# RWKV block inverse: products of 64x64 in two quarters of the array in place of block-diagonal products of 128x128

## The chip, the core and the metric

The kernel runs on one core of a Trainium2 chip. The metric is the time of one execution in device microseconds. The engines are named as in the profile: PE is TensorE's matrix products, PEld its loads of weights, DVE is VectorE, ACT is ScalarE, POOL is GpSimd, SP is SyncE, which issues the transfers. TensorE's array has 128 rows and 128 columns; rows belong to the partitions of the operands, columns to the partitions of the result. A product whose operands stand in partitions 0 to 63 and whose result goes to partitions 0 to 63 uses one quarter of the array; one from 64 to 127 into 64 to 127 uses the opposite quarter.

## The reference

Two model blocks follow each other over 512 tokens of width 1024. The first is a convolution and an attention layer with their feed-forward layers, the second mixes three things (sliding attention, attention to a memory, and RWKV) and has a feed-forward layer behind it. The change concerns the RWKV mixer alone: six heads of 64 channels, over each of which runs a recurrence of a 64x64 state.

```
def rwkv7_scan(r, w, k, v, a, bvec):
    decay = jnp.exp(-jnp.exp(w))
    def step(state, inp):
        r_t, d_t, k_t, v_t, a_t, b_t = inp
        sa = jnp.einsum('bhvk,bhk->bhv', state, a_t)
        state = (state * d_t[:, :, None, :] + sa[..., None] * b_t[:, :, None, :]
                 + v_t[..., None] * k_t[:, :, None, :])
        return state, jnp.einsum('bhvk,bhk->bhv', state, r_t)
    _, y = lax.scan(step, s0, xs)
```

Around it: `w`, `a` and the gate come from small projections, the result is normalized per head, scaled, gets a bonus term, is multiplied by the gate, and goes through the rows of `w_out` that belong to it.

## The kernel before

The kernel is one program that a scheduler orders. Instructions of each engine are taken in an order that comes from the order in the code, priorities and modelled times; buffers are handed out in that order too. All products here are of fp32 operands, and TensorE does each of them as two instructions, each with its load of weights.

The recurrence is done in chunks of 64 tokens. Eight chunks make the 512 tokens; two chunks make a block of 128 tokens, so there are four blocks (`b`), and two chunks (`q`) in each. Six heads are worked on as three pairs (`i` is the pair, `e` the head in the pair). For each pair:

- `prep(i)` makes the operands: two projections (L1212, L1216), activations and exponentials on ScalarE (with loads of tables in between: L1214, L1218, L1223, L1234), a scan, and transposes (L1264).
- `grams(i)` makes for every block four matrices of 64x64 for each chunk by products of 64 rows (L1398), and takes them out of PSUM under a mask (L1401). The mask writes them as block-diagonal 128x128 matrices: chunk 0 in the upper left, chunk 1 in the lower right, zeros elsewhere. So each block and head has a tile NM of 128x512. L1404 makes a product with one of them, L1402 and L1403 on GpSimd prepare the matrix to be inverted and the start of its inverse XT, and L1409 transposes XT into X.
- `level(o, l)`, five times, doubles the size of the blocks already inverted. For each head three groups of four products, one for each block, 128x128 by 128x128: P1 (L1424: NM by X, taken out under a mask as T by VectorE, L1425), P2 (L1430: XT by T, taken out as the new X by ScalarE, L1432; not in the last level) and P3 (L1436: T by XT, taken out as the new XT by VectorE, L1438).
- `finish(i)` applies the inverse (L1445), makes the chunks' transition matrices (L1454, L1461 to L1463), runs the recurrence over chunks (L1479 and L1480, six steps, each a product and an operation on VectorE), adds up the output in one bank of PSUM (L1485, L1487, L1492), and normalizes it (L1494 to L1517).

The work around it sets the order: `w_out_attention` (products into `wo`, lines L161 to L165 by its helper) stands early in the code with low priority, and fills TensorE beside the first pair's levels. The second pair's levels run beside the first pair's `finish`, the third pair's beside the second's; the last `finish` has nothing beside it. `w_out_add` multiplies the three pairs' results by their rows of `w_out`, which `w_out` loads into NM buffers and splits in two (L1543 to L1547). PSUM has banks `mm` (2), `aux` (2), `rw` (3) and `wo` (1) in this part. The masks stand in one constant array (`rwc`).

Of the kernel before, what the change touches and what calls it, by code (L numbers as in the profile page):

```python
# [57 lines left out]
def _build(ctx, tc, ins, out, stop, dbg):  # L58
# [1213 lines left out]
    with sub("e_x", "xp"), sub("e_w", "wp"), sub("e_t", "sm"):  # L1272
# [34 lines left out]
        for n, (name, i) in enumerate(order):  # L1307
# [12 lines left out]
            if name in ("l", "r", "k", "v"):  # L1320
                shifted(u, {"r": 0, "k": 3, "v": 6, "l": 9}[name] + i, lora if name == "l" else rkv[name][i])
                if n == PREPN:
# [5 lines left out]
                    for c, w in ((640, 512), (1152, 448), (1600, 384)):  # L1328
                        rc.append(tmp()[:, :w])
                        sp.dma_start(out=rc[-1], in_=ins["rwc"][:, c : c + w])  # L1330
                    m4k, eye64, pair = rc[0], rc[1][:, 0:64], rc[1][:, 64:192]
                    lev = [rc[1][:, 192 + 128 * i : 320 + 128 * i] for i in range(2)] + [rc[2][:, 128 * i : 128 * i + 128] for i in range(3)]
# [44 lines left out]
    def rw():  # L1377
        return ps(512, tag="rw")

    def nmt(dt=F32):  # L1380
        return wk(512, "NM", 18, dt=dt)

    def grams(i, o):
        o.NM, o.X, o.XT = [], [], []
        for e in range(2):
            hr = slice(64 * e, 64 * e + 64)
            NM = []
            XT = wk(512, f"XT{e}", 3)
            pk = ps(256, tag="aux")
            for b in range(4):  # L1390
                c = slice(b * 128, (b + 1) * 128)
# [3 lines left out]
                for x, s in ((o.kt, 0), (o.bt, 128)):  # L1395
                    for q in range(2):
                        ch = slice(b * 128 + 64 * q, b * 128 + 64 * q + 64)
                        pe.matmul(p[64 * q : 64 * q + 64, s : s + 128], x[hr, ch], o.AR[hr, b, :, 64 * q : 64 * q + 64], start=True, stop=True)  # L1398
# [6 lines left out]
                NM.append(nm)  # L1405
            X = wk(512, f"X{e}", 2)
            pt = rw()
            for b in range(4):
                pe.transpose(pt[:, b * 128 : (b + 1) * 128], XT[:, b * 128 : (b + 1) * 128], ident)  # L1409
            act.copy(out=X, in_=pt)  # L1410
            act.copy(out=o.RH[:, :, e, 64:128], in_=pk.rearrange("p (t c) -> p t c", t=4))
# [304 lines left out]
```

## Time and profile before

| what | value |
|---|---|
| median of three runs | 2374.22 us (2371.76 to 2375.54) |
| profiled execution | 2373.74 us |
| its span | 2372.0 us |
| TensorE busy (PE) | 2279.0 us, 96% |
| VectorE busy (DVE) | 1644.5 us, 69% |
| ScalarE busy (ACT) | 942.7 us, 40% |
| GpSimd busy (POOL) | 170.9 us, 7% |
| chain that ended last | PE 88%, DVE 5%, ACT 3%, DMA 2% |

The span runs from the first to the last instruction that the profile shows; 1.74 us lie around it. A busy TensorE is not one at its peak, since products overlap in it: how long a group of products takes is read from the start of one group to the start of the next. RWKV work stands between about 1736 and 1993 us, a ninth of the span.

### The profile page before, as it was taken

The numbers are of one execution on the slowest core, as the hardware profiler recorded it, in microseconds if no ns is written. First come the engines' busy times: TensorE is split into PE (matmuls) and PEld (weight loads), VectorE is DVE, ScalarE is ACT, GpSimd is POOL, SyncE is SP. The second block draws the span as 40 slices with busy tenths as digits, with TensorE's granted clock in tenths as the row PEclk, the third lists the DMA queues.
The fourth block names the chain that finished last, engine by engine and source line by source line (L and its number), as shares of the span: only waits on it lengthen the run. The fifth ranks groups of instructions, "written<-read, shape, count | busy, mean of one in ns | idle before, by whom it ended". The sixth has DMA issues, their size and how long they took to land.

```text
span 2372.0 us, 34287 instructions
## 1 busy us (share of the span) xinstructions
PE 2279.0 (96%) x13910; PEld 1885.8 (80%) x13910; DVE 1644.5 (69%) x2634; ACT 942.7 (40%) x1616; POOL 170.9 (7%) x246
## 2 busy tenths in 40 slices
PE   5999899999999999899999999998989999999999
PEld 2777588888888888766789999987768786788887
DVE  4889769867677768666687777676645546767666
ACT  3222633223332235566653433355633323433332
POOL 0000000000000000344300000001431100000000
PEclk8999999999999999999999999999999999999999
DMA  8455323323233211421132322222200002232221
GB/s 314 168 206 172 139 115 116 124 99 107 90 128 112 98 54 55 129 68 36 54 118 78 124 74 106 72 73 68 66 23 23 5 28 105 87 106 90 89 89 54
DMA packets 51385, 229.02 MB, mean 97 GB/s; under 512 B 6395, under 2 KB 11164, under 8 KB 32796
## 3 DMA queue, kind: packets, MB, share of 16 engines
q1 hardware_dynamic: 51228, 226.84, 27.8%
q8 instruction: 109, 1.79, 0.3%
q14 instruction: 48, 0.39, 0.1%
HBM read 213.84 MB, written 6.68 MB: 93 GB/s over the span
## 4 chain that ended last, share of the span: by engine, by line
PE 88%; DVE 5%; ACT 3%; DMA 2%; issue 1%; POOL 0%; SPq 0%; DVEq 0%; ACTq 0%; POOLq 0%
PE mm L161 23%; PE mm L163 23%; PE mm L165 23%; PE po L909 1%; PE aux L905 1%; PE mm L576 1%; PE rw L1436 1%; PE rw L1430 1%; PE rw L1424 1%; DMA raw<-in_ada 1%; PE aux L370 1%; PE sc L887 1%; PE mm L783 1%; PE sc L888 1%; PE aux L402 1%
## 5 line engine op out<-in xcount | busy, mean ns | idle before, releaser
L161 PE MATMUL mm<-xh,wh 128*128 128x512 f32 (+2 forms) x2336 | 658.4, 338 | 15.2 <-ACT xh L479 4.7
L163 PE MATMUL mm<-xl,wh 128*128 128x512 f32 (+2 forms) x2336 | 660.9, 337 | 3.1 <-DVE xl L219 2.1
L165 PE MATMUL mm<-xh,wl 128*128 128x512 f32 (+2 forms) x2336 | 659.7, 337 | 1.9 <-DVE wl L144 1.9
L143 ACT ACTIVATE wh<-raw 128x1024 fp32r<-128x1024 f32 x263 | 274.8, 1057 | 543.3 <-PE mm L163 491.9
L161 PEld LDWEIGHTS mm<-xh,wh 128*128 128x128 f32 x2336 | 409.5, 190 | 70.5 <-ACT xh L479 6.8
L163 PEld LDWEIGHTS mm<-xl,wh 128*128 128x128 f32 x2336 | 410.8, 190 | 55.5 <-DVE xl L219 3.1
L165 PEld LDWEIGHTS mm<-xh,wl 128*128 128x128 f32 x2336 | 410.7, 190 | 49.2 <-DVE wl L144 2.8
L144 DVE TENSOR_TENSOR wl<-raw,wh 128x1024 fp32r<-128x1024 f32 x263 | 324.2, 1242 | 44.5 <-ACT wh L143 40.0
L161 PE MATMUL mm<-gh,wh 128*128 128x512 f32 (+1 forms) x704 | 253.7, 368 | 2.2 <-ACT gh L288 2.0
L163 PE MATMUL mm<-gl,wh 128*128 128x512 f32 (+1 forms) x704 | 254.8, 368 | 0.0
L165 PE MATMUL mm<-gh,wl 128*128 128x512 f32 x704 | 254.0, 367 | 0.0
L249 DVE TENSOR_TENSOR u<-mm,R 128x256 f32<-128x256 f32 x88 | 37.5, 426 | 178.5 <-PE mm L165 176.7
L161 PEld LDWEIGHTS mm<-gh,wh 128*128 128x128 f32 x704 | 131.3, 188 | 26.1 <-ACT gh L288 2.4
L165 PEld LDWEIGHTS mm<-gh,wl 128*128 128x128 f32 x704 | 131.3, 189 | 23.4
L163 PEld LDWEIGHTS mm<-gl,wh 128*128 128x128 f32 x704 | 131.3, 189 | 23.0 <-DVE gl L289 0.3
L310 DVE SCALAR_TENSOR_TENSOR hl<-mm,mod,hl 128x512 f32<-128x512 f32 x176 | 131.3, 747 | 21.1 <-PE mm L165 20.5
L288 ACT ACTIVATE gh<-cv 128x512 fp32r<-128x512 f32 (+1 forms) x66 | 46.5, 705 | 243.0 <-DVE cv L286 243.0
L271 DVE SCALAR_TENSOR_TENSOR cv<-u,vec,cv 128x512 f32<-128x512 f32 (+1 forms) x132 | 110.4, 837 | 9.9 <-ACT cv L262 9.2
L553 DVE SCALAR_TENSOR_TENSOR accp<-v,dwt,accp 128x798 f32<-128x798 f32 (+2 forms) x118 | 113.9, 975 | 2.6
L272 DVE SCALAR_TENSOR_TENSOR cv<-u,vec,cv 128x512 f32<-128x512 f32 (+1 forms) x132 | 110.6, 839 | 3.1
L284 ACT ACTIVATE cv<-cv 128x512 f32<-128x512 f32 (+1 forms) x66 | 46.4, 704 | 118.2 <-DVE cv L272 118.0
L396 DVE SCALAR_TENSOR_TENSOR ac<-ra,sc,ac 128x512 f32<-128x512 f32 x112 | 81.8, 744 | 1.4 <-DMA ra<-in_ada 1.4
(470 smaller groups left out, 3092.2 us busy)
## 6 DMA issues: line engine op xcount, KB each, us to landing
raw<-in_up SPq DMA_DIRECT2D x63, 1024.0 KB, 4.9
raw<-in_dn SPq DMA_DIRECT2D x33, 1024.0 KB, 4.8
raw<-in_ada SPq DMA_DIRECT2D x24, 1024.0 KB, 6.3
ra<-in_ada SPq DMA_DIRECT2D x48, 512.0 KB, 3.6
raw<-in_pw SPq DMA_DIRECT2D x12, 1024.0 KB, 6.2
S<-vd SPq DMA_DIRECT2D x28, 407.0 KB, 5.0
raw<-in_w_in SPq DMA_DIRECT2D x17, 512.0 KB, 3.5
raw<-in_qkv SPq DMA_DIRECT2D x6, 1024.0 KB, 5.0
```

The source lines that it names most:

```text
L143: act.activation(out=hi, in_=part, func=AF.Copy)
L144: dve.tensor_tensor(out=lo, in0=part, in1=hi, op=ALU.subtract)
L161: pe.matmul(p, whi[:, c], xhi[:, s], start=first, stop=False)
L163: pe.matmul(p, whi[:, c], xlo[:, s], start=False, stop=False)
L165: pe.matmul(p, wlo[:, c], xhi[:, s], start=False, stop=last)
L271: dve.scalar_tensor_tensor(out=cv[:, 0:CW], in0=u[:, 0:CW], scalar=wv[0], in1=cv[:, 0:CW], op0=ALU.mult, op1=ALU.add)
L272: dve.scalar_tensor_tensor(out=cv[:, 0:CW], in0=u[:, 2 : 2 + CW], scalar=wv[2], in1=cv[:, 0:CW], op0=ALU.mult, op1=ALU.add)
L284: act.activation(out=ca[:, 0:CW], in_=ca[:, 0:CW], func=AF.Silu)
L288: act.activation(out=gh[:, 0:CW], in_=cb[:, 0:CW], func=AF.Copy)
L310: dve.scalar_tensor_tensor(out=hs, in0=p, scalar=g2[i][:, m : m + 1], in1=hs, op0=ALU.mult, op1=ALU.add)
L396: dve.scalar_tensor_tensor(out=a, in0=t[:, q, :], scalar=sc2[:, k, n : n + 1], in1=a, op0=ALU.mult, op1=ALU.add)
L553: dve.scalar_tensor_tensor(out=acc[:, a:b], in0=x, scalar=w, in1=acc[:, a:b], op0=ALU.mult, op1=ALU.add)
```

## The change

The two chunks of a block are no longer put into one block-diagonal matrix. Chunk 0 stays in partitions 0 to 63, chunk 1 in 64 to 127, both in the same 64 columns, so T, X, XT, the masks and the gram matrices are half as wide (256 columns for four blocks instead of 512; one NM tile of 128x1024 for a head instead of four of 128x512). Each product of 128x128 becomes two of 64x64, one in the upper left quarter of the array and one in the lower right. `bq` lists the eight chunks with their partitions. `grams` takes its products out of PSUM two blocks at a time, GpSimd prepares a head's four blocks at once, and the transposes become products with the identity. In `finish`, products over both chunks become one for each; Q and the output of even and odd chunks get tiles of their own, and the part of the output that needs the state (L1492 before, L1496 after) has its own tile `pc` in a bank of `rw`, which is added on VectorE. `w_out` loads its weights in one piece of 1024 columns.

```diff
@@ grams
+    hs = [slice(0, 64), slice(64, 128)]
+    bq = [(b, hs[q], slice(b * 64, b * 64 + 64)) for b in range(4) for q in range(2)]
...
-                nm = nmt()
-                both = p.rearrange("p (m c) -> p m c", c=64).unsqueeze(2).to_broadcast([128, 4, 2, 64])
-                dve.tensor_tensor(out=nm.rearrange("p (m q c) -> p m q c", m=4, q=2), in0=both, in1=m4k.rearrange("p (m q c) -> p m q c", m=4, q=2), op=ALU.mult)
-                pool.tensor_tensor(out=nm[:, 256:384], in0=nm[:, 256:384], in1=ident, op=ALU.add)
-                pool.tensor_tensor(out=XT[:, c], in0=nm[:, 256:384], in1=pair, op=ALU.mult)
-                pe.matmul(pk[:, b * 64 : (b + 1) * 64], nm[:, 0:128], o.VT[:, b * 128 + 64 * e : b * 128 + 64 * e + 64], start=True, stop=True)
...
-                pe.transpose(pt[:, b * 128 : (b + 1) * 128], XT[:, b * 128 : (b + 1) * 128], ident)
+                if b % 2:
+                    dve.tensor_tensor(out=nm[:, b * 256 - 256 : b * 256 + 256].rearrange("p (b x) -> p b x", b=2), in0=p2.rearrange("p (b x) -> p b x", b=2),
+                                      in1=m4k.unsqueeze(1).to_broadcast([128, 2, 256]), op=ALU.mult)
+            pool.tensor_tensor(out=NM[:, :, 2], in0=NM[:, :, 2], in1=eye64.unsqueeze(1).to_broadcast([128, 4, 64]), op=ALU.add)
+            XT = wk(256, f"XT{e}", 3)
+            pool.tensor_tensor(out=c4(XT), in0=NM[:, :, 2], in1=pair.unsqueeze(1).to_broadcast([128, 4, 64]), op=ALU.mult)
+            for b, r, c in bq:
+                pe.matmul(pk[r, c], NM[r, b, 0], o.VT[r, b * 128 + 64 * e : b * 128 + 64 * e + 64], start=True, stop=True)
...
+            for b, r, c in bq:
+                pe.matmul(pt[r, c], XT[r, c], ident[r, r], start=True, stop=True)
@@ level
-                pe.matmul(p[:, c], NM[b][:, 256:384], X[:, c], start=True, stop=True)
-            dve.tensor_tensor(out=v4(T), in0=v4(p), in1=lev[l].unsqueeze(1).to_broadcast([128, 4, 128]), op=ALU.mult)
+                pe.matmul(p[r, c], NM[r, b, 2], X[r, c], start=True, stop=True)
+            dve.tensor_tensor(out=c4(T), in0=c4(p), in1=lev[l].unsqueeze(1).to_broadcast([128, 4, 64]), op=ALU.mult)
...
-                    pe.matmul(p[:, c], XT[:, c], T[:, c], start=True, stop=True)
-                o.X[e] = wk(512, f"X{e}", 2)
+                    pe.matmul(p[r, c], XT[r, c], T[r, c], start=True, stop=True)
+                o.X[e] = wk(256, f"X{e}", 2)
...
-                pe.matmul(p[:, c], T[:, c], XT[:, c], start=True, stop=True)
-            o.XT[e] = wk(512, f"XT{e}", 3)
+                pe.matmul(p[r, c], T[r, c], XT[r, c], start=True, stop=True)
+            o.XT[e] = wk(256, f"XT{e}", 3)
@@ finish
-                pe.matmul(pq[hs[e], c], G[e][:, b, 0:64], o.NM[e][b][:, 384:512], start=True, stop=True)
+                pe.matmul(pq[n % 2][hs[e], c], G[e][r, b, 0:64], o.NM[e][r, b, 3], start=True, stop=True)
...
-                pe.matmul(py[hs[e], c], G[e][:, b, 64:128], o.NM[e][b][:, 384:512], start=True, stop=False)
+                pe.matmul(py[n % 2][hs[e], c], G[e][r, b, 64:128], o.NM[e][r, b, 3], start=True, stop=False)
...
-                        pe.matmul(py[hs[e], nn], S[hs[e], nn], QT[hs[e], nn], start=False, stop=n % 2 == 1)
-        act.copy(out=y, in_=py)
+        for q in range(2):
+            act.copy(out=half(y, q), in_=c4(py[q]))
+        pc = rw()
+        for n in range(1, 8):
+            for e in range(2):
+                pe.matmul(pc[hs[e], n * 64 : n * 64 + 64], S[hs[e], n * 64 : n * 64 + 64], QT[hs[e], n * 64 : n * 64 + 64], start=True, stop=True)
+        dve.tensor_tensor(out=y[:, 64:512], in0=pc[:, 64:512], in1=y[:, 64:512], op=ALU.add)
@@ w_out
-            raw = nmt()
-            sp.dma_start(out=raw, in_=ins["w_ob"][n][:, c * 512 : (c + 1) * 512])
+        raw, hi, lo = nmt(), nmt(F32R), nmt(F32R)
+        sp.dma_start(out=raw, in_=ins["w_ob"][n])
```

Line numbers move by a few: after the change P1 is L1430, P2 L1435 and P3 L1440, the recurrence's product is L1482, its part of the output L1496.

The scheduler orders the new program anew. TensorE in the first pair's levels, between two runs of `w_out_attention` products (`wo`); before:

```order
L165 MATMUL wo<-oh,wl 128x512
L1430 MATMUL rw<-T_16731,XT_16708 128x128 x4
L1436 MATMUL rw<-XT_16708,T_16731 128x128 x4
L1424 MATMUL rw<-X_16722,NM 128x128 x4
L161 MATMUL wo<-oh,wh 128x512
L163 MATMUL wo<-ol,wh 128x512
```

The same place of the changed program:

```order
L165 MATMUL wo<-oh,wl 128x512
L1435 MATMUL rw<-T_16747,XT_16712 64x64 x8
L1440 MATMUL rw<-XT_16712,T_16747 64x64 x8
L1430 MATMUL rw<-X_16734,NM 64x64 x8
L1264 MATMUL aux<-ident,AR 128x128 x4
L1264 MATMUL aux<-ident,bt 128x128 x4
L161 MATMUL wo<-oh,wh 128x512
```

The three groups of a level still stand together between two runs of wide products; each has eight products of 64x64 in place of four of 128x128.

TensorE where the second pair's levels run beside the first pair's recurrence (`aux<-f` is a step of it, `f` are its tiles); before, products of 128x128 and of 64x64 alternate:

```order
L1430 MATMUL rw<-T_17304,XT_16963 128x128 x4
L1436 MATMUL rw<-XT_16963,T_17304 128x128 x2
L1479 MATMUL aux<-f 64x64 x2
L1436 MATMUL rw<-XT_16963,T_17304 128x128 x2
L1424 MATMUL rw<-X_17051,NM 128x128 x4
L1479 MATMUL aux<-f 64x64 x2
L1492 MATMUL mm<-f 64x64 x2
L1430 MATMUL rw<-T_17325,XT_17011 128x128 x4
L1436 MATMUL rw<-XT_17011,T_17325 128x128 x4
L1424 MATMUL rw<-X_17316,NM 128x128 x2
L1479 MATMUL aux<-f 64x64 x2
L1492 MATMUL mm<-f 64x64 x2
```

After the change, from the point where the first two steps have been done:

```order
L1496 MATMUL rw<-f 64x64 x4
L1430 MATMUL rw<-X_17100,NM 64x64 x8
L1482 MATMUL aux<-f 64x64 x2
L1496 MATMUL rw<-f 64x64 x2
L1435 MATMUL rw<-T_17440,XT_17089 64x64 x8
L1440 MATMUL rw<-XT_17089,T_17440 64x64 x5
L1482 MATMUL aux<-f 64x64 x2
L1496 MATMUL rw<-f 64x64 x2
L1440 MATMUL rw<-XT_17089,T_17440 64x64 x3
L1430 MATMUL rw<-X_17145,NM 64x64 x8
L1482 MATMUL aux<-f 64x64 x2
L1496 MATMUL rw<-f 64x64 x2
```

All rows here are now of 64x64, and the steps of the recurrence are set between or into the groups of a level.

VectorE in the last `finish`, from Q (L1465, L1469 after) to the subtraction of the mean (L1497, L1500 after); L1547 is a split of `w_out` weights, L1480 (L1483 after) a step of the recurrence; before:

```order
L1465 TENSOR_TENSOR f<-mm,AR 128x512
L1469 TENSOR_TENSOR f<-mm,t 128x4x64
L1474 TENSOR_TENSOR f<-mm,lend 128x4x64
L1469 TENSOR_TENSOR f<-mm,t 128x4x64
L1474 TENSOR_TENSOR f<-mm,lend 128x4x64
L1547 TENSOR_TENSOR NM<-NM 128x512
L1480 SCALAR_TENSOR_TENSOR f<-aux,lend,f 128x64 x3
L1547 TENSOR_TENSOR NM<-NM 128x512
L1480 SCALAR_TENSOR_TENSOR f<-aux,lend,f 128x64 x3
L1497 SCALAR_TENSOR_TENSOR f<-mm,f 128x512
```

After:

```order
L1469 TENSOR_TENSOR f<-rw,AR 128x4x64 x2
L1472 TENSOR_TENSOR f<-mm,t 128x4x64
L1477 TENSOR_TENSOR f<-mm,lend 128x4x64
L1472 TENSOR_TENSOR f<-mm,t 128x4x64
L1477 TENSOR_TENSOR f<-mm,lend 128x4x64
L1483 SCALAR_TENSOR_TENSOR f<-aux,lend,f 128x64 x6
L1497 TENSOR_TENSOR f<-rw,f 128x448
L1500 SCALAR_TENSOR_TENSOR f<-mm,f 128x512
```

The two splits have moved ahead, to the levels before, and the 448-column add (L1497 after) has come in behind the last step.

## Rows read from the trace of the kernel before

**Rows 1.** Stretches of RWKV work: busy us of each engine (instructions), granted TensorE clock, DMA.

```profile
1755.00:1833.50 78.50, 75.50 (x535) 63.87 (x535) 45.23 (x68) 26.21 (x46) 18.99 (x33) 0.98 0.10 30
1833.50:1863.30 29.80, 28.30 (x319) 24.97 (x319) 9.16 (x19) 5.18 (x10) 0.00 (x0) 1.00 0.03 11
1863.30:1867.90 4.60, 4.56 (x26) 2.92 (x25) 1.67 (x3) 1.22 (x2) 0.00 (x0) 1.00 0.00 0
1867.90:1901.40 33.50, 29.50 (x218) 23.85 (x218) 20.43 (x35) 15.52 (x23) 8.29 (x13) 0.93 0.00 1
1901.40:1932.20 30.80, 30.07 (x340) 26.53 (x339) 13.86 (x27) 8.95 (x16) 2.69 (x6) 0.97 0.17 53
1932.20:1952.70 20.50, 17.44 (x134) 15.14 (x133) 12.08 (x18) 4.82 (x8) 0.00 (x0) 1.00 0.00 1
1952.70:1969.40 16.70, 14.40 (x215) 12.15 (x214) 5.80 (x14) 2.65 (x5) 0.00 (x0) 1.00 0.05 18
```

**Rows 2.** Groups of instructions, 1735 to 1995 us: busy us, mean ns of one, idle before.

```profile
L1425 DVE TENSOR_TENSOR T<-rw,t 128x512 f32<-128x512 f32 x30 | 20.7, 690 | 12.5 <-PE rw L1424 12.1
...
L1462 PE MATMUL mm<-T,q 64*64 64x64 f32 x64 | 8.5, 218 | 0.0
...
L1404 PE MATMUL aux<-q,NM 128*128 128x64 f32 x32 | 6.2, 281 | 2.9 <-DVE NM L1401 2.9
...
L1469 DVE TENSOR_TENSOR f<-mm,t 128x256 f32<-128x256 f32 x6 | 2.5, 423 | 9.8 <-PE mm L1463 9.8
...
L1411 ACT COPY RH<-aux 128x256 f32<-128x256 f32 x6 | 2.2, 370 | 13.0 <-PE aux L1404 12.9
```

**Rows 3.** Chain that ended last, third pair's levels: start us, us, what.

```profile
1937.57 1.13 PE rw L1430 x8
1938.70 0.89 PE rw L1436 x8
1939.60 0.91 PE rw L1424 x8
...
1940.53 0.70 DVE T L1425
...
1941.36 1.13 PE rw L1430 x8
```

**Rows 4.** TensorE in order of time, last recurrence: start, from first start to last end.

```profile
1963.84 0.33 PE L1479 MATMUL aux<-f 64*64 64x64 f32 x4 [0.39 <-DVE f L1480]
...
1964.56 0.33 PE L1479 MATMUL aux<-f 64*64 64x64 f32 x4 [0.27 <-DVE f L1480]
1964.72 0.28 PE L1492 MATMUL mm<-f 64*64 64x64 f32 x4
1964.93 0.44 PE L1485 MATMUL mm<-NM,T 128*64 128x128 f32 x4
1965.20 0.39 PE L1487 MATMUL mm<-NM,q 128*64 128x128 f32 x4
1965.52 0.33 PE L1479 MATMUL aux<-f 64*64 64x64 f32 x4
1965.69 0.28 PE L1492 MATMUL mm<-f 64*64 64x64 f32 x4
```

**Rows 5.** TensorE in order of time, products of one quarter behind each other.

```profile
1956.01 0.28 PE L1462 MATMUL mm<-T,q 64*64 64x64 f32 x2
1956.13 0.28 PE L1463 MATMUL mm<-q 64*64 64x64 f32 x2
```

**Rows 6.** TensorE in order of time, second pair's grams.

```profile
1815.79 0.78 PE L1404 MATMUL aux<-VT,NM 128*128 128x64 f32 x6
```

**Rows 7.** Chain that ended last, from `prep` of the third pair to its grams.

```profile
1869.09 1.28 ACT L1214
...
1880.14 0.19 ACT rn L1234
...
1891.93 0.58 PE mm L1398 x8
```

More of the change, by code (lines that the diff above doesn't have):

```diff
@@ L1327, in _build @@
                     rc = []
-                    for c, w in ((640, 512), (1152, 448), (1600, 384)):
+                    for c, w in ((640, 512), (1152, 192)):
                         rc.append(tmp()[:, :w])
                         sp.dma_start(out=rc[-1], in_=ins["rwc"][:, c : c + w])
-                    m4k, eye64, pair = rc[0], rc[1][:, 0:64], rc[1][:, 64:192]
-                    lev = [rc[1][:, 192 + 128 * i : 320 + 128 * i] for i in range(2)] + [rc[2][:, 128 * i : 128 * i + 128] for i in range(3)]
+                    m4k, eye64, pair = rc[0][:, 0:256], rc[0][:, 256:320], rc[0][:, 320:384]
+                    lev = [rc[0][:, 384 + 64 * i : 448 + 64 * i] for i in range(2)] + [rc[1][:, 64 * i : 64 * i + 64] for i in range(3)]
                 if name == "l":
@@ L1443, in finish @@
             p = rw()
-            for b in range(4):
-                pe.matmul(p[:, b * 128 : (b + 1) * 128], o.XT[e][:, b * 128 : (b + 1) * 128], o.RH[:, b, e], start=True, stop=True)
-            g = wk(512, f"T{e}", 2)
+            for b, r, c in bq:
+                pe.matmul(p[r, b * 128 : (b + 1) * 128], o.XT[e][r, c], o.RH[r, b, e], start=True, stop=True)
+            g = wk(512, f"G{e}", 1)
             act.mul(out=g, in_=p, mul=-1.0)
             G.append(v4(g))
-        hs = [slice(0, 64), slice(64, 128)]
-        pq, pzx = ps(512), [ps(512), ps(512)]
-        for b in range(4):
-            c = slice(b * 128, (b + 1) * 128)
+        half = lambda x, q: x.rearrange("p (b q c) -> p b q c", b=4, q=2)[:, :, q]
+        pq, pzx = [rw()[:, 0:256] for _ in range(2)], [ps(512), ps(512)]
+        for n, (b, r, c) in enumerate(bq):
             for e in range(2):
-                pe.matmul(pq[hs[e], c], G[e][:, b, 0:64], o.NM[e][b][:, 384:512], start=True, stop=True)
+                pe.matmul(pq[n % 2][hs[e], c], G[e][r, b, 0:64], o.NM[e][r, b, 3], start=True, stop=True)
         for e in range(2):
@@ L1464, in finish @@
         QT = ftmp()
-        dve.tensor_tensor(out=v4(QT), in0=v4(pq), in1=o.AR[:, :, 1], op=ALU.add)
+        for q in range(2):
+            dve.tensor_tensor(out=half(QT, q), in0=c4(pq[q]), in1=o.AR[:, :, 1, 64 * q : 64 * q + 64], op=ALU.add)
         AT = ftmp()
-        half = lambda x, q: x.rearrange("p (b q c) -> p b q c", b=4, q=2)[:, :, q]
         for q in range(2):
@@ L1538, in w_out @@
     def w_out(n, x):
-        hi, lo = [], []
-        for c in range(2):
-            raw = nmt()
-            sp.dma_start(out=raw, in_=ins["w_ob"][n][:, c * 512 : (c + 1) * 512])
-            hi.append(nmt(F32R))
-            lo.append(nmt(F32R))
-            act.activation(out=hi[c], in_=raw, func=AF.Copy)
-            dve.tensor_tensor(out=lo[c], in0=raw, in1=hi[c], op=ALU.subtract)
+        raw, hi, lo = nmt(), nmt(F32R), nmt(F32R)
+        sp.dma_start(out=raw, in_=ins["w_ob"][n])
+        act.activation(out=hi, in_=raw, func=AF.Copy)
+        dve.tensor_tensor(out=lo, in0=raw, in1=hi, op=ALU.subtract)
         return hi, lo, x
@@ L1553, in w_out_add @@
             for i, (hi, lo, x) in enumerate(parts):
[L1554 removed]
+                mm3([(p, slice(0, 512))], (hi, lo), x, i == 0, i == len(parts) - 1, m * 128)
             dve.tensor_tensor(out=hl[m], in0=p, in1=hl[m], op=ALU.add)
```

62 lines of the change are left out of this document (26 added, 36 removed).

## The prediction

> **What bounds the kernel now.** I read the stretches of the RWKV part first, then the groups of its instructions, then the chain that ended last, and last the order of time on TensorE, where a start tells more than a busy time does. Only the RWKV part (1755 to about 1993 us) changes; what comes after it starts earlier by what this part saves. There TensorE is busy 75.5 of 78.5 us up to the first `finish`, 28.3 of 29.8 and 30.07 of 30.8 in the two stretches in which `finish` runs beside the next pair's levels, but 17.44 of 20.5 and 14.4 of 16.7 us towards the end [rows 1]. So two limits alternate: TensorE's own work, and the wait between two products in which VectorE takes T out of PSUM. The chain shows that wait plainly: eight instructions each of L1430 (P2), L1436 (P3) and L1424 (P1) in 1.13, 0.89 and 0.91 us, then 0.70 us of L1425 (T) with nothing else on the chain, and the next P2 3.79 us after the last [rows 3].
>
> **What the change is worth in TensorE time.** A product of fp32 is two instructions. A group of four 128x128 products (8 instructions) holds TensorE 0.89 us [rows 3], 0.11 us an instruction. After, the group is 16 instructions of 64x64 with 64 columns. In one quarter of the array two such instructions together last 0.28 us where one lasts 0.218 [rows 2, 5]: they start 0.06 us apart, and pairs follow each other 0.117 us apart [rows 5], 0.058 us an instruction. The question is whether the two chunks, which sit in opposite quarters (rows and columns 0 to 63, rows and columns 64 to 127), run at once. L1492 already does this with its two heads: four instructions, two in each of two opposite quarters, also last 0.28 us [rows 4], so the four start within the same 0.06 us: the second quarter costs nothing. A group of 16 is then 8 pairs by 0.058 = 0.47 us, against 0.89: 0.42 less. There are 3 pairs of heads x 2 heads x (5 + 4 + 5) = 84 such groups in `level`: **35.5 us**. In `grams`, six of L1404's 128x64 instructions last 0.78 us, one 0.28 [rows 2, 6], so 0.10 us from one to the next; 6 groups of 8 become 16 quarter instructions, 0.80 to 0.47: **2 us**. The transposes L1409 (4 instructions, 0.45 us) become 16 quarter ones (0.47), and L1445, L1454, L1485 and L1487 keep their time, since half the rows doubles their number: nothing.
>
> **Changes of shape.** When TensorE goes from one shape of weights to another it pays. L1487's four instructions of 128x64, 0.27 us after L1485's four, are followed by the 64x64 of L1479 after 0.32 us instead of 0.22 (four instructions in two pairs, 0.11 a pair); L1479's four take 0.17 instead of 0.117; and from L1492 to L1485 pass 0.21 instead of 0.117 [rows 4]. So a change costs about 0.10 us before and 0.05 behind it, 0.15 in all. I expected more of them, since the levels leave the shape of the wide products around them. The order says the opposite: from the first gram product to the first `w_out_add` product 131 changes become 69, because now `grams`, `level`, `finish` and the state recurrence all have one shape (up to the first `finish` 39 become 35, between the first and second 45 become 24, then 32 and 7, 15 and 3). 62 x 0.15 = **9 us**. TensorE's work falls by 46.5 us in all.
>
> **The evictions.** T and XT go from 512 columns in 0.690 us (L1425) to 256, X likewise; 256 columns cost 0.423 us on VectorE (L1469) and 0.370 on ScalarE (L1411) [rows 2]. NM's 24 evictions become 12 of the same 512 columns. This frees some 24 us of VectorE, which is not the bound; it counts only where T is waited for. There the cycle of a head and level is P2 1.13 (0.89 and 0.24 of a late first instruction and its tail), P3 0.89, P1 0.91, T 0.70 and 0.16 of hand-overs, 3.79 us [rows 3]. After: P2 0.47 + 0.24, P3 0.47, P1 0.48, T 0.42 and 0.16, **2.25 us**.
>
> **What it adds.** `y` is now copied before the recurrence ends, and a 448-column add (estimate 0.6 us, between 0.423 and 0.690 [rows 2]) takes the place of the last copy (128x512 on ScalarE, estimated 0.6 us from the 0.370 of 256 columns): nothing. `pc` holds one of the three `rw` banks while the recurrence runs; the levels beside it have two, so P1 waits for ScalarE's copy of X behind P2: 0.71 + 0.37 + 0.16 = 1.24 us where P2 and P3 together take 0.55 + 0.47. That is 0.2 us a cycle, three cycles in each of two stretches: 1.3 us at most, 0 at least (where T is late anyway); I take 0.7 in each. GpSimd's 48 short operations become 12 of 256 columns in two steps behind all of a head's NM; the `w_out_attention` products stand behind them in the first pair, the last levels of the pair before in the others. The w_ob loads and casts are all ahead of the third pair's levels, where two casts stood in the last recurrence on VectorE: some of the 16.7 us there, not counted apart.
>
> **The sum, by stretch** [rows 1]. *To the first finish, 78.5 us*: TensorE-bound with `w_out_attention` as filler. 28 groups x 0.42 + 4 gram groups x 0.33 + 4 changes x 0.15 = 13.7, and the two last waits for T get shorter: 14. *finish beside the levels, 29.8 us*: L1445 1.75 (16 instructions at 0.11), L1454 0.9 (8), 48 products of L1461 to L1463 x 0.117 = 5.6, L1485 and L1487 1.9 (pairs of quarters 0.117 apart), then P1 and three cycles with the recurrence in them 0.5 + 6.75, the add and its hand-overs 1.5, the last gap 0.7 of `rw`: 19.6. Saves 10. *4.6 us to the next pair's L1212*: the two 512-column products stay (2.1), 2.5 groups become one: saves 1.7. *33.5 us to the second finish*: here the savings go. From L1212 on, ScalarE has nothing but tables and activations one behind another from 1869.09 to 1880.33, and VectorE's chain of operand preparation runs to 1891.93 [rows 7]. Neither is halved; only five T and XT evictions in it (0.27 each) and one P2 and P3 (0.42 each) are: saves 2.2, although TensorE has 8 us less to do. *30.8 us*: as the 29.8, and more groups move behind it: 19.6, saves 11. *20.5 us*: more levels are left for this stretch (19 groups instead of 14): two wide products 2.1, L1502 and L1510 1.4, four groups and two changes of shape 2.3, a T with its hand-overs 1.2, four cycles 9.0, the last P3, P1 and T 1.8, the last XT 0.6: 18.4, saves 2.1. *16.7 us*: no filler; 1.75 + 0.9 + 5.6 + 1.9 + 4.5 steps of the recurrence at 0.72 (from one L1479 to the next [rows 4]) + 1.5 = 15: saves 1.7. `w_out_add` behind it is unchanged. Together 42.6.
>
> From this I take 2 us for the clock: it was 1.00 in most stretches and 0.93 and 0.97 in two [rows 1], and the stretch behind L1212 will have TensorE idle for a third of it. So 41 us. The profiled execution, 2373.74 us (span 2372.0 and 1.74 around it), becomes 2332.7; the median of the three runs is 0.5 above it: **2333 us**.
>
> **Rivals.** *The recurrence and T waits eat more* (chance 14 in 100). If the stretches behind the first `finish` follow their chains and get only the evictions, about 0.27 us in each of some 25 waits, 7 us, and half of the saved changes, 4 us, with the 14 of the first stretch: 25 us, 2349. For it: these stretches already have idle TensorE at the end. Against: 28.3 of 29.8 and 30.07 of 30.8 us were work.
>
> *The two quarters do not run at once* (5 in 100). 16 instructions of 0.058 are 0.93 us, 0.04 more than now: 84 x 0.04 = 3 us lost, the changes of shape give 9, T waits 4: 2364. L1492 speaks against it, though it shows runs of four instructions, and now runs of 16 to 80 follow. The Trainium skill's page TensorEngine Tiling (Array Packing), section Restrictions and Gotchas, says that different row tiles cannot access the same PSUM bank at the same time. By that rule this rival would hold, as both chunks of a block go to the same bank here, and the time would be the 2364 above. L1492 writes both its quarters to one bank, with the times above, so the trace does not bear the rule out.
>
> *Slower* (3 in 100). A stretch made only of quarter products might let TensorE's clock fall to 1.2 GHz. Behind the first `finish` about 65 us of TensorE's work would be of that kind (56 groups x 0.47, three times 11.8 in `finish`, 4 in `grams`); at half the clock it takes 65 more, of which some 15 fall into waits: 50 against 41 saved, 2383. It decides from some 40 us lost, so the clock would have to be low nearly all the way. Against it: the 16.7 us before `w_out_add` hold 148 quarter instructions (48 products of L1461 to L1463, 12 of L1479, 14 of L1492, two each) among 215, and idle gaps, at 1.00 [rows 1].
>
> **Chances.** Forecast, 2319 to 2346: 73. Chains: 14. No concurrency: 5. Slower: 3. More than forecast (the chains shorten too, below 2319): 5. A change that cannot be measured, within 0.2% or 4.7 us, which is about what this kernel's runs can tell: none of the cases gives it; 1 in 100 stays. Faster by more 0.96, same 0.01, slower 0.03. The range 2319 to 2352 holds the forecast's own range and the chains rival; it leaves out the other 13 and a tail.
>
> **What would show it.** The level groups of 16: 0.47 us from start to start, T in 0.42, XT in 0.42, X in 0.37. The last levels cycle in 2.25 us instead of 3.79. The first `finish` starts 14 us earlier and takes 10 us less to its end, but the way from the next L1212 to the second `finish` stays at 31 us or more. Groups of 0.9 us would make the forecast wrong at its root; granted clocks near 0.5 behind the first `finish` would make it slower; a T that waits behind other VectorE work would bring the chains rival.

## The result, and the profile after

The changed kernel takes 2332.76 us (median of 4 runs, 2327.18 to 2335.13) against 2374.68 for the kernel before on the same chip: 0.9822 of it, 95% interval 0.9807 to 0.9837, 41.9 us less. The forecast was 2333. The profiled executions stand further apart, 2372.0 and 2325.4 us of span, but 3.2 of these 46.6 us were already there at 1755 us, ahead of the changed part. The total is as forecast, but several terms of the sum are not, and cancel.

The stretches of the changed kernel, cut at the events that cut [rows 1], and behind them w_out_add, up to its last addition (columns as in [rows 1]):

```profile
1751.80:1813.50 61.70, 60.25 (x827) 49.09 (x828) 33.45 (x59) 23.82 (x46) 8.79 (x9) 0.99 0.16 47
1813.50:1828.90 15.40, 13.66 (x426) 13.06 (x420) 6.32 (x18) 3.58 (x10) 0.00 (x0) 1.00 0.12 39
1828.90:1831.80 2.90, 2.90 (x27) 1.26 (x23) 1.07 (x2) 0.77 (x2) 0.00 (x0) 1.00 0.00 0
1831.80:1868.20 36.40, 29.80 (x463) 24.05 (x464) 21.14 (x39) 17.93 (x29) 7.59 (x7) 0.81 0.01 3
1868.20:1886.30 18.10, 15.13 (x425) 14.43 (x421) 7.47 (x19) 4.56 (x10) 0.00 (x0) 0.91 0.16 59
1886.30:1905.60 19.30, 14.35 (x323) 11.84 (x324) 10.89 (x22) 4.30 (x10) 0.00 (x0) 1.00 0.01 2
1905.60:1918.20 12.60, 9.96 (x285) 9.00 (x279) 4.92 (x14) 2.08 (x5) 0.00 (x0) 0.95 0.02 4
1918.20:1947.60 29.40, 28.00 (x89) 18.32 (x89) 15.19 (x24) 7.18 (x12) 0.10 (x1) 0.79 0.00 0
```

The last stretch in the kernel before:

```profile
1969.40:1993.50 24.10, 22.43 (x89) 14.94 (x89) 15.04 (x24) 7.17 (x12) 0.10 (x1) 1.00 0.00 1
```

| stretch | before, us | after, us | saved | forecast |
|---|---|---|---|---|
| to the first finish | 78.5 | 61.7 | 16.8 | 14 |
| first finish beside the levels | 29.8 | 15.4 | 14.4 | 10 |
| to the next L1212 | 4.6 | 2.9 | 1.7 | 1.7 |
| L1212 to the second finish | 33.5 | 36.4 | -2.9 | 2.2 |
| second finish beside the levels | 30.8 | 18.1 | 12.7 | 11 |
| the last levels | 20.5 | 19.3 | 1.2 | 2.1 |
| the last finish | 16.7 | 12.6 | 4.1 | 1.7 |
| w_out_add | 24.1 | 29.4 | -5.3 | 0 |
| sum | 238.5 | 195.8 | 42.7 | 42.6 |

From the 42.6 the forecast then took 2 us for the clock, without a place. The three long stretches in which TensorE was the bound saved more than forecast, and two stretches became longer. In both of these the granted clock is low: 0.81 and 0.79, against 0.93 and 1.00 before. 0.79 over 29.4 us means that 2 x 0.21 x 29.4 = 12.3 us of them ran at 1.2 GHz.

The groups that the levels are made of, in the changed kernel (columns as in [rows 2]):

```profile
L1442 DVE COPY XT<-rw 128x256 f32<-128x256 f32 x30 | 12.6, 421 | 15.4 <-PE rw L1440 14.5 <-PE rw L1430 0.8
L1431 DVE TENSOR_TENSOR T<-rw,t 128x256 f32<-128x256 f32 x30 | 12.6, 421 | 1.8 <-PE rw L1430 1.3
L1437 ACT COPY X<-rw 128x256 f32<-128x256 f32 x24 | 8.9, 370 | 34.2 <-PE rw L1435 33.9
```

and the chain that ended last through one head of the third pair's levels, which answers to [rows 3]:

```profile
1898.99 0.68 PE rw L1435 x16
1899.67 0.47 PE rw L1440 x16
1900.14 0.48 PE rw L1430 x16
1900.64 0.44 DVE T L1431
1901.22 0.68 PE rw L1435 x16
```

A group of 16 takes 0.47 or 0.48 us, T 0.42, and from one P2 to the next pass 2.23 us: the forecast's 0.47, 0.42 and 2.25, against 3.79 before.

The chain behind the third pair's L1212, where 2.9 us were lost:

```profile
1832.99 1.28 ACT L1214
...
1841.42 1.87 PE aux L1232 x8
1843.28 1.05 PE rw L1435 x16
1844.34 0.85 PE rw L1440 x16
...
1855.80 0.05 PE mm L1403
...
1863.34 1.24 DVE NM L1546
...
1864.61 0.56 DVE NM L1405
...
1867.09 0.55 POOL XT L1409
...
1867.69 0.68 PE rw L1416 x16
```

Between 1843 and 1846, at a clock of 0.50, a group of 16 takes 0.85 us, where it takes 0.48 at full clock. Even so, the way from the load of L1214's table to the first gram product is as long as before: 22.8 us, from 1832.99 to 1855.80 (L1403) here and from 1869.09 to 1891.93 (L1398) in [rows 7]. So the low clock may have kept the forecast's 2.2 us from coming, but the 2.9 us are lost behind the first gram product, where the clock was 1.00 again. There, at 1863.34, VectorE does a cast of w_out's weights (L1546, the subtraction that makes their second half) while the last NM of the grams (L1405) stands behind it in its queue; GpSimd's second step, behind that NM, is the last thing that the transposes (L1416) wait for. TensorE is idle there for 1.24 us, until that NM, and for 2.02, until that step. GpSimd in order of time shows that step for the first head and, beside VectorE's next cast (1865.41 to 1867.05), for the second:

```profile
1861.48 0.73 POOL L1409 TENSOR_TENSOR XT<-NM,t 128x256 f32<-128x256 f32 x1
...
1866.05 1.58 POOL L1409 TENSOR_TENSOR XT<-NM,t 128x256 f32<-128x256 f32 x1
```

The cut itself has moved, too. In the kernel before, 17 of TensorE's instructions of the grams (8 of L1398, 6 of L1404, 3 of L1409) stand behind the first product of the second finish, which starts at 1901.46; from start to start they and the gaps at their changes of shape take 2.2 us there. Four of them:

```profile
1904.65 0.44 PE L1398 MATMUL mm<-AR,kt 64*64 64x128 f32 x4
```

After the change all of the grams stand ahead of it. So about 2 us of the 2.9 lost, and of the 12.7 saved in the second finish, are work that went from one row of the table to the other. The two rows together hold what counts: 64.3 us became 54.5, 9.8 saved where 13.2 were forecast.

### The profile page after: what moved, and what is told of

Its sections match the earlier page's. It is cut to its first block, busy times and chain, and to the rows that moved or that the text cites. A ratio compares the mean times of both kernels' runs of the same rounds, so it can differ in the third digit from the quotient of the medians.

```text
span 2325.4 us, 36202 instructions
## 1 busy us (share of the span) xinstructions
PE 2230.1 (96%) x14894; PEld 1843.8 (79%) x14894; DVE 1622.7 (70%) x2625; ACT 935.1 (40%) x1616; POOL 158.0 (7%) x210
## 4 chain that ended last, share of the span: by engine, by line
PE 87%; DVE 5%; ACT 3%; DMA 2%; issue 1%; SPq 0%; POOL 0%; DVEq 0%; ACTq 0%; POOLq 0%
PE mm L161 24%; PE mm L163 24%; PE mm L165 23%; PE po L909 2%; PE aux L905 1%; PE mm L576 1%; DMA raw<-in_ada 1%; PE aux L370 1%; PE sc L887 1%; PE rw L1440 1%; PE mm L783 1%; PE rw L1435 1%; PE sc L888 1%; PE aux L402 1%; PE rw L1430 1%
```

## The experiments

Times of whole runs differ by 3 to 12 us for one kernel, but most stretches come back: in a second execution of the changed kernel seven of the eight differ by at most 0.1 us, and the first by 0.7 (62.4 us, at a clock of 0.98). The first scatters more, up to 65.2 us at 0.95 in kernels in which nothing in it was edited. So the experiments are read by stretches first, and by medians second.

**The changed kernel again.** No edit.

> The changed kernel once more, unaltered, as the one that the next kernels are compared with, and to see whether its two stretches of half clock come back. If the clock falls because TensorE has too little to do there, it falls again at the same two places (behind the third pair's L1212, and in the last recurrence up to the first products of w_out_add), some 13 us each, and the time is 2333 us (2327 to 2336). If it was chance in the one profiled execution, it is gone or elsewhere, and w_out_add takes 24 us from L1499 to its last addition in place of 29.

Measured: 2330.74 us (0.9814, 0.9799 to 0.9828). The stretch behind L1212 took 36.42 us and w_out_add 29.4, at clocks of 0.81 and 0.79. The low clock at the two places is a property of this kernel.

**One quarter after the other.**

```diff
+    qb = bq[0::2] + bq[1::2]
@@ level, in each of its three groups
-            for b, r, c in bq:
+            for b, r, c in qb:
```

> The products of each group in level are issued for the four chunks of one quarter first and then for the four of the other, in place of alternating. If the two quarters run at once only where their instructions stand next to each other, a group of 16 takes 0.93 us in place of 0.47, and 84 groups give 39 us more work; nearly all of it on the path, so 2363 to 2372 us, little better than before the change. If the gain comes from the narrower evictions and the fewer changes of shape, it stays within 5 us of 2333.

Measured: 2349.58 us (0.9882, 0.9860 to 0.9904), 18.8 more than the changed kernel: half of the 39, and four times the 5 of the rival. TensorE in order of time shows why (start, from first start to last end; L1436 is P2 here, L1441 P3):

```profile
1918.56 0.76 PE L1436 MATMUL rw<-T,XT 64*64 64x64 f32 x13 [0.61 <-DVE T L1432]
1919.10 0.27 PE L1441 MATMUL rw<-XT,T 64*64 64x64 f32 x1
1919.16 0.22 PE L1436 MATMUL rw<-T,XT 64*64 64x64 f32 x1
...
1919.68 0.27 PE L1431 MATMUL rw<-X,NM 64*64 64x64 f32 x1
```

The next group's first quarter starts while the second quarter of the group ahead is still at work: P3 starts 0.54 us behind P2, P1 0.58 behind P3, not 0.93. So quarters run at once not only when their instructions stand side by side; the engine reaches some instructions ahead. The Trainium skill's page TensorE: Matmul & The Clock Gate, section Part 3: Packing small matmuls — row/col tiling, has matmuls start strictly in the order of the program; here all of P2 stands ahead of P3 on the engine, and the first of P3 starts at 1919.10, one of P2 at 1919.16, so the trace differs. A group costs 0.1 us more (84 x 0.1 = 8 us), and T waits for the end of a group behind which no other follows, by the overlap seen some 0.2 us later (both estimates). The 18.8 us are not products alone: in the profiled execution, the fastest of the four (2340.74 us), the second finish and the last levels ran at 0.78 and 0.86 in place of 0.91 and 1.00. At equal clocks, the first stretch took 66.8 us in place of 61.7 to 62.4, and the first finish 17.0 in place of 15.4. These two alone lose 6 us or more, so the rival that the gain is not in the products falls.

**Evictions as wide as before.**

```diff
-            dve.tensor_tensor(out=c4(T), in0=c4(p), in1=lev[l].unsqueeze(1).to_broadcast([128, 4, 64]), op=ALU.mult)
+            dve.tensor_tensor(out=T2.rearrange('p (h b c) -> p h b c', h=2, c=64), in0=c4(p).unsqueeze(1).to_broadcast([128, 2, 4, 64]), in1=lev[l].unsqueeze(1).unsqueeze(1).to_broadcast([128, 2, 4, 64]), op=ALU.mult)
-                act.copy(out=o.X[e], in_=p)
+                act.copy(out=X2.rearrange("p (h c) -> p h c", h=2), in_=p.unsqueeze(1).to_broadcast([128, 2, 256]))
-            dve.tensor_copy(out=o.XT[e], in_=p)
+            dve.tensor_copy(out=XT2.rearrange("p (h c) -> p h c", h=2), in_=p.unsqueeze(1).to_broadcast([128, 2, 256]))
```

> The changed kernel with products of 64x64, but T, X and XT taken out of PSUM as 512 columns (each of the 256 written twice), as wide as before. By the prediction's step on evictions a T takes 0.69 in place of 0.42 us, and X 0.59 in place of 0.37, on the way only where TensorE waits for them, some 25 places: 5 to 9 us more than the changed kernel, 2338 to 2342. If evictions are what the change is worth, 20 us or more are lost; if they are hidden everywhere, it stays at 2333.

Measured: 2343.18 us (0.9862, 0.9841 to 0.9883), 12.4 more, above the 5 to 9 expected. The levels beside the first finish show what the wait itself costs at a clock of 1.00, 16.7 us in place of 15.4; those beside the second took 20.2 in place of 18.1, but at 0.86 in place of 0.91. The last levels grew by 5.8, to 25.1, but at a clock of 0.75 in place of 1.00. So the longer wait itself is part of the 12.4, and a lower clock another part; how much each, these runs don't tell.

**Q in another bank, in the kernel before.** The products of `finish` (L1461 to L1463) took less in the changed kernel than I had counted, so the edit that might do it was tried alone.

```diff
-        pq, pzx = ps(512), [ps(512), ps(512)]
+        pq, pzx = rw(), [ps(512), ps(512)]
```

> The kernel before, with one edit: Q (L1454) goes to a bank of rw instead of mm, so that both banks of L1461 to L1463 are free at once and the scheduler alternates the two row halves. If products of different row halves into different banks run at once, the 48 products of each finish take 2.8 us in place of 5.6, where TensorE is the bound: 5 to 8 us less than before, 2366 to 2369. If they don't overlap, or the levels wait for the bank that Q takes, 2374 or a little more.

Measured: 2375.55 us against 2376.84 (0.9993, 0.9981 to 1.0004): nothing. But the stretches say that it does what it should. The first finish, L1212 to the second finish, the last finish and w_out_add (columns as in [rows 1]):

```profile
1830.90:1854.40 23.50, 22.86 (x299) 20.11 (x300) 8.38 (x18) 4.61 (x9) 0.00 (x0) 1.00 0.04 13
...
1858.90:1894.70 35.80, 32.48 (x239) 26.74 (x239) 21.64 (x36) 15.98 (x24) 8.29 (x13) 0.90 0.01 1
...
1947.00:1963.10 16.10, 12.36 (x215) 9.99 (x213) 5.81 (x14) 2.65 (x5) 0.00 (x0) 0.97 0.05 18
1963.10:1992.50 29.40, 28.16 (x89) 18.45 (x89) 15.19 (x24) 7.17 (x12) 0.10 (x1) 0.78 0.00 1
```

The first finish takes 23.5 us in place of 29.8, and TensorE is busy 2 us less in the last one; then w_out_add runs at 0.78 and takes 29.4 in place of 24.1, and 35.8 us instead of 33.5 pass from L1212 to the second finish, at 0.90 instead of 0.93. The second finish gained nothing (31.2 us in place of 30.8, at 0.96 in place of 0.97). In w_out_add, whose work is the same, what was saved came back as low clock. Not all of the first finish's 6.3 us are these products: 20 fewer of TensorE's instructions stand in it.

**The old order of these products, in the changed kernel.**

```diff
-            for n in range(8):
+            for n in (0, 2, 4, 6, 1, 3, 5, 7):
                 cr, b = hs[n % 2], n // 2
```

> The changed kernel with the 48 products of L1464 to L1466 in the order of the kernel before: for each head the four chunks of one row half, then the four of the other. If the two row halves run at once only where they alternate, the products (96 instructions in 3.32 us now) go back towards 5.6 us, some of it hidden where instructions of the other half stand close behind: the two stretches from the first product of finish to L1499 with levels beside them (15.43 and 18.09 us) grow by 1.0 to 2.3 us each, and the last one (12.57) too. If the order on the engine makes no difference, they stay within 0.1 us, as in the changed kernel's second execution.

Measured (one execution, 2340.0 us): the 96 instructions take 5.4 us; first finish 16.9 us, last one 14.8 (15.4 and 12.6), the second 18.2, but at a clock of 1.00 in place of 0.91. TensorE in order of time, in the changed kernel:

```profile
1870.28 0.22 PE L1465 MATMUL mm<-G,BT 64*64 64x64 f32 x1
1870.34 0.22 PE L1464 MATMUL mm<-BT,G 64*64 64x64 f32 x1
1870.34 0.22 PE L1466 MATMUL mm<-VT,KT 64*64 64x64 f32 x1
```

and in this one:

```profile
1877.70 0.28 PE L1464 MATMUL mm<-BT,G 64*64 64x64 f32 x2
1877.82 0.28 PE L1465 MATMUL mm<-G,BT 64*64 64x64 f32 x2
```

Alternating, two instructions start in 0.055 us, otherwise in 0.117, as in [rows 5]. These products write the same columns from different rows of the array, into two banks.

**Extra products in the last recurrence.** They are computed and never read; the rest is unchanged.

```diff
+        pd = ps(512, tag="wo") if i == 2 else None
...
+            if pd is not None:
+                pe.matmul(pd[:, 0:128], blk1, S[:, n * 64 : n * 64 + 64].unsqueeze(1).to_broadcast([128, 2, 64]), start=True, stop=True)
...
+        if pd is not None:
+            pe.matmul(pd[:, 0:256], blk1, S[:, 448:512].unsqueeze(1).to_broadcast([128, 4, 64]), start=True, stop=True)
```

> The changed kernel with work that nobody needs: behind each of the six steps of the last recurrence one fp32 product of 128x128 (into the bank of w_out_attention, which is free then, never read), and one of 256 columns behind the last. In the changed kernel the clock was at half for 13.7 us from the middle of this recurrence into w_out_add, and w_out_add took 29.2 us in place of 24.2. If idle gaps bring the clock down, the extra work of some 2 us keeps it up: 3 to 5 us less than the changed kernel (2331 here), 2326 to 2328. If the clock falls for another reason (the shape of the products, or what came earlier), the extra products only cost up to 1.5 us: 2331 to 2333.

The last finish and w_out_add of this kernel:

```profile
1910.90:1924.70 13.80, 12.88 (x296) 11.11 (x292) 4.92 (x14) 2.08 (x5) 0.00 (x0) 1.00 0.02 4
1924.70:1948.90 24.20, 22.48 (x89) 14.99 (x89) 15.10 (x24) 7.19 (x12) 0.10 (x1) 1.00 0.00 0
```

TensorE is busy 2.9 us more in the first, which costs 1.2 us; the clock stays at 1.00, and w_out_add takes 24.2 us in place of 29.4. The six stretches ahead are as in the changed kernel. So the clock stays up when TensorE has more to do in the recurrence, and the clock is the whole loss in w_out_add: 4.0 us less over both. The whole runs don't resolve it: 2331.66 us (2324.52 to 2335.04; 0.9808, 0.9778 to 0.9839). In the changed kernel the fall comes at 1917, behind the last step of the recurrence (1916.4), not in its middle.

Too little work in the recurrence is not the whole condition, though. In the kernel with one quarter after the other the last finish has the same instructions in the same order as in the changed kernel, and TensorE is as idle in it; its clock, which had been low in the last levels (0.86), stays up here and in w_out_add:

```profile
1923.90:1936.50 12.60, 9.98 (x283) 9.08 (x280) 4.93 (x14) 2.09 (x5) 0.00 (x0) 1.00 0.02 4
1936.50:1960.70 24.20, 22.51 (x89) 14.97 (x89) 15.08 (x24) 7.19 (x12) 0.10 (x1) 1.00 0.00 0
```

So what went before counts as well; which part of it, no run shows. The extra products also differ in shape from the quarter products around them, and amount and shape were not tried apart. Quarter products alone are not what the fall needs: the kernel before with Q moved still has L1485 and L1487 of 128 rows in its last recurrence, and its clock fell too.

**Extra products behind L1212 too.** In `prep` of the third pair, one behind each of four activations, with the kernel above for the rest.

```diff
+        def warm(t):
+            if pd is not None:
+                pe.matmul(pd[:, 0:256], blk1, t[:, 0:256], start=True, stop=True)
...
+        warm(sw)
+        warm(a)
+        warm(lam)
+        warm(q)
```

> As the kernel with extra products in the last recurrence, and four more extra products (128x256, on the results of the activations in prep of the third pair) in the stretch behind L1212, where the clock is at half for 13.7 us of 36.42. If TensorE's short idle times there bring the clock down, and the extra work covers them: 33.5 to 34.5 us in this stretch, and 23.5 behind the last L1499 as in the kernel with the last recurrence filled alone. If the fall is decided before the first extra product can run (the clock was at half from 1835.4, and the first activation ends at 1834.97), the stretch stays at 36.4 us or grows by up to 1 us.

Measured (one execution, 2327.01 us): 37.1 us for the stretch, at 0.82; w_out_add again 24.2. TensorE worked 2.8 us more there and nothing came of it: a miss for the half that covers the idle time, a hit for the other, that the first extra product comes too late. What brings the clock down in this stretch is left open.

**w_out_add of the first two pairs ahead of the last finish.**

```diff
+    with tc.high_priority(offset=WPRI):
+        w_out_add([w_out(n, (obh[n], obl[n])) for n in (0, 1)], tag="wo")
     for l in range(5):
         level(st[2], l)
     finish(2, st[2])
-    w_out_add([w_out(n, (obh[n], obl[n])) for n in (0, 1)])
```

> The part of w_out_add that needs only the first two pairs (48 products, 11 us) moves to the bank of w_out_attention, in front of the third pair's levels in the code and with low priority; the order puts it between the last six groups of levels and ahead of the last finish, none inside the recurrence. TensorE was idle for 7.6 of the 31.8 us from the second finish's L1499 to the last finish's end, and what came behind it ran at half clock. If the waits for T can be filled: 5 to 8 us less than 2331, 2323 to 2326. Against it: that part also fills the normalization behind the last recurrence, where then TensorE is idle, and the clock falls as before; then 2329 or more.

Its last levels, last finish and what is left of w_out_add:

```profile
1889.40:1912.60 23.20, 21.80 (x351) 16.46 (x351) 13.73 (x27) 4.35 (x10) 0.00 (x0) 1.00 0.01 2
1912.60:1929.30 16.70, 14.51 (x300) 11.87 (x296) 7.12 (x18) 2.09 (x5) 0.10 (x1) 1.00 0.01 2
1929.30:1949.00 19.70, 15.01 (x41) 8.86 (x41) 9.74 (x16) 7.53 (x12) 0.00 (x0) 0.65 0.00 0
```

The last levels and the last finish take 3.9 and 4.1 us more, the rest of w_out_add 9.7 less, and this end runs at 0.65. 2333.76 us (0.9815, 0.9795 to 0.9835): a gap filled in one place is a gap opened behind it.

**Casts behind the last NM.** First by late loads, then by buffers that come free late for the rounded halves only.

```diff
-        raw, hi, lo = nmt(), nmt(F32R), nmt(F32R)
+        raw = prp.tile([128, 1024], F32, tag=("RH", "AR")[n], name="raw") if n < 2 else nmt()
+        hi, lo = nmt(F32R), nmt(F32R)
```

> The w_ob weights of the first two pairs are loaded into two buffers that become free only in the second finish, so their casts can't stand ahead of the last NM of the third pair's grams. If the wait of VectorE for ScalarE's cast and the cast itself (1863.34 to 1864.58) hold up the NM behind them, the stretch from L1212 to the second finish loses 2.3 us of its 36.4; the casts then cost up to 1 us beside the recurrence: 1.5 to 2.5 us less than 2331, about 2329. If they are covered, it stays within 1 us of 2331.

Measured: 2339.16 us (0.9836, 0.9812 to 0.9861), 8 worse. To the second finish 33.7 us, as expected, and then 28.6 in place of 18.1. The chain there (L1547 is the cast):

```profile
1874.45 3.25 DMA raw<-in_w_ob
1877.72 1.07 ACT NM L1546
1878.81 1.22 DVE NM L1547
1880.03 0.68 DVE f L1469 x2
```

VectorE's Q (L1469) now waits behind a cast that waits for its load.

```diff
-        raw, hi, lo = nmt(), nmt(F32R), nmt(F32R)
+        raw, lo = nmt(), nmt(F32R)
+        hi = prp.tile([128, 1024], F32R, tag=("RH", "AR")[n], name="hi") if n < 2 else nmt(F32R)
```

> The w_ob weights of the first two pairs are loaded as early as in the changed kernel, but their rounded halves go to the two buffers that become free in the second finish, so that the casts stand behind the last NM and behind the products that read those buffers, with the data long there. If the wait for a cast in front of the last NM costs 2.3 us and the earlier attempt failed only because the loads came too late: from the third pair's L1212 to the second finish 33.7 to 34.2 us in place of 36.42, and the stretch behind it within 1 us of 18.09. If VectorE has no room there either, that stretch grows by 1.2 us for each cast.

Measured (one execution, 2340.03 us): 33.9 us to the second finish, at 0.85, then 21.9, at 0.77. The first half as expected, the second worse than 1 us; over both 1.3 us are lost, with clock and casts mixed in it. Both edits together, the late loads and the early w_out_add:

> Both edits together, the early w_out_add of two pairs and the late w_ob loads. If both work and do not meet in the same gap: 2320 to 2324. If the loads now come too late for the early w_out_add, no better than the better of the two alone.

Measured: 2338.89 us (0.9838, 0.9818 to 0.9857): no better than the worse of the two.

**GpSimd's steps for two blocks at a time,** in the kernel with extra products in the last recurrence.

```diff
-            pool.tensor_tensor(out=NM[:, :, 2], in0=NM[:, :, 2], in1=eye64.unsqueeze(1).to_broadcast([128, 4, 64]), op=ALU.add)
-            pool.tensor_tensor(out=c4(XT), in0=NM[:, :, 2], in1=pair.unsqueeze(1).to_broadcast([128, 4, 64]), op=ALU.mult)
@@ behind each NM
+                    h = slice(b - 1, b + 1)
+                    pool.tensor_tensor(out=NM[:, h, 2], in0=NM[:, h, 2], in1=eye64.unsqueeze(1).to_broadcast([128, 2, 64]), op=ALU.add)
+                    pool.tensor_tensor(out=c4(XT)[:, h], in0=NM[:, h, 2], in1=pair.unsqueeze(1).to_broadcast([128, 2, 64]), op=ALU.mult)
```

> The kernel with extra products in the last recurrence, and GpSimd's two steps of grams done for two blocks at a time, each behind its own NM, in place of once for four blocks behind the last. In the changed kernel TensorE waits 2.02 us for GpSimd's second step (it took 1.58 us beside VectorE's cast) before the last transposes. If that wait is what the wide steps cost: 35.0 to 35.7 us in place of 36.42 from the third pair's L1212 to the second finish, other stretches as in the kernel without this edit, 23.5 us behind the last L1499; the RWKV part 4.5 to 5.5 us shorter than in the changed kernel, 2325 to 2329 us. If the wait belongs to the cast ahead of the last NM and not to GpSimd's steps, the stretch stays within 0.3 us of 36.42 and the time is that of the kernel without this edit.

Three of its stretches, the last of them the second finish:

```profile
1756.00:1823.10 67.10, 64.98 (x829) 51.11 (x829) 32.44 (x58) 24.32 (x46) 10.58 (x15) 0.92 0.14 44
...
1841.90:1876.50 34.60, 29.57 (x456) 23.84 (x456) 20.94 (x39) 17.96 (x29) 9.17 (x11) 0.80 0.01 2
1876.50:1895.00 18.50, 15.53 (x435) 14.84 (x429) 7.47 (x19) 4.57 (x10) 0.10 (x1) 0.91 0.17 60
```

From L1212 to the second finish 34.6 us at nearly the clock of the changed kernel (36.4 at 0.81), 1.8 less, and 0.4 more in the stretch behind it (18.5 in place of 18.1): the wide steps on GpSimd cost some 1.4 us there. But the first stretch took 67.1 us in place of the 62.3 of the kernel without this edit, at a clock of 0.92 in place of 0.98, and the whole is 2332.26 us (0.9812, 0.9799 to 0.9826), as the changed kernel and above the 2325 to 2329 expected. That the 4.8 us of the first stretch are clock and not the edit is likely, not shown: the kernel with late loads has the same order on TensorE as the changed kernel, and took 65.1 us there, at 0.95.

## Why the prediction was right

*Products.* Right, by the step it rests on: opposite quarters run at once, 0.48 us a group. The rival without concurrency did not come. The Trainium skill's page TensorEngine Tiling (Array Packing), section Restrictions and Gotchas, says that different row tiles cannot access the same PSUM bank at the same time. The trace differs: both quarters of a group write one bank here, and 16 instructions that take 0.058 us each in one quarter took 0.48.

*Evictions and cycle.* Right: 0.42 for T, 2.23 us a cycle. Beside the recurrence the chain of the changed kernel shows P2 again after 2.42 us, the size of the forecast's 2.25 and 0.2, but not for its reason:

```profile
1823.05 0.68 PE rw L1435 x16
...
1824.02 0.05 PE aux L1482
...
1824.99 0.44 DVE T L1431
1825.47 0.68 PE rw L1435 x16
```

The forecast had P1 wait for ScalarE's copy of X, since `pc` holds a bank. TensorE waits for no such copy in this stretch or in the second finish. Four products of the recurrence (L1482, L1496) stand among those of P3 and make the cycle longer; here the sum was right by luck.

*The finish.* The step "48 products of L1461 to L1463 x 0.117 = 5.6" was mis-sized in all three stretches: they take 3.3 us, and Q's 32 instructions run among them. The diff showed the cause, Q moved from `mm` to `rw`, and I read it as a move of a tile; it frees the second bank that the other row half waits for. 2.3 us are its products alone, and near 3 with Q's 0.9: the greater part of the 4.4 us that the first finish saved beyond 10, and enough for the 2.4 of the last. The second had the same gain in these products; its 12.7 hold some 2 us of grams that left it, and its clock was 0.91.

*The stretch behind L1212.* "Saves 2.2" became 2.9 lost, some 2 of them by the cut; over this stretch and the second finish 3.4 us less were saved than forecast. Up to the first gram product nothing was saved. At 1.2 GHz three groups of 0.85 to 1.05 us stand in front of L1241 there; whether they ate the 2.2 is not shown. Behind it, the step "the w_ob loads and casts are all ahead of the third pair's levels" saw where they went and priced them only as a gain; one stands ahead of the last NM, and without it the stretch takes 33.7 us in place of 36.4. And "GpSimd's 48 short operations become 12", counted at nothing, cost some 1.4 us, as the last experiment shows; I had not asked what VectorE does beside them: a step took 1.58 us beside such a cast, and 0.73 without. The Trainium skill's page SBUF — State Buffer, section SBUF: two separate sides, says that a VectorE operation with two inputs in SBUF and a GpSimd one that reads SBUF shut each other out for a whole instruction. The trace agrees: the step of 1.58 us begins while the cast runs and ends 0.58 us behind it.

*The clock.* "I take 2 us" was too small. w_out_add alone lost 5.3 us, all of it clock, as the extra products show. The rival "slower" named the clock, but with stretches made only of quarter products as its cause. The first such stretch ran at 1.00 (15.4 us), the second at 0.91, and the two long falls lie elsewhere; more work in the recurrence takes one of them away, and what brings the other is open.

*The first stretch* saved 16.8 in place of 14; I did not take the 2.8 apart. Nor does any run take apart the 9 us that the forecast gave to changes of shape. These errors cancel: 9.6 us more saved up to and in the first finish and in the last one, 3.4 less over the stretch behind L1212 and the second finish, 5.3 less in w_out_add, 0.9 less in the last levels. The total was met for that reason as much as for the mechanism. Two slips of its arithmetic change nothing: its savings by stretch add up to 42.7 and not 42.6, and its chances to 101 in 100.

## What to carry to other kernels

Before a saving in TensorE's work is booked, ask what TensorE does in the time that it gains: where nothing fills it, the clock may fall, and the work behind it, unchanged, takes the saving back (29.4 us for 24.1). A tile that moves to another PSUM bank changes who else can run: list the tiles that shared the old bank. Read small edits in stretches between the same two events, most of which repeat to 0.1 us in this kernel, not in whole runs that scatter by 3 us and more. And see that the same work lies between the two events in both kernels: here 17 gram instructions changed sides.

## What the runs showed of the hardware

- Instructions of two row halves of the array that write the same columns into two PSUM banks run at once if they alternate: 96 in 3.3 us, against 5.4 in order of halves.
- Issued one quarter after the other, groups still overlap by some instructions: 0.54 to 0.58 us from group to group, not the 0.93 of no overlap.
- Useless products shortened what follows: 2.9 us more of TensorE's work, 4.0 us less time over two stretches. The same last finish without them brought the clock down in the changed kernel (w_out_add at 0.79) and left it up in another (1.00).
- A GpSimd operation of 128x256 took 1.58 us beside a VectorE subtraction of 128x1024, 0.73 without.
